# Block products of an MLP on one NeuronCore: another order of the products, operands split next to their use

## The chip, the cores and the metric

One core of a Trainium2 chip runs the kernel; the other cores are idle. The metric is the device time of one execution in microseconds (us). TensorE multiplies (moving operands stream through a stationary one, results in PSUM banks), VectorE and ScalarE work on tiles in SBUF and PSUM, SyncE (SP) issues the DMA transfers. Each engine works through its instructions in the order in which they stand in its queue, and waits where one needs something that isn't there.

## The reference, cut to what matters

```python
def reference(x, ..., w_out, norm_mlp_w, w_mlp_up, w_mlp_down, norm_final_w):
    ...
    h = h + mixed @ w_out
    hn = _rmsnorm(h, norm_mlp_w)
    h = h + jnp.square(jax.nn.relu(hn @ w_mlp_up)) @ w_mlp_down
    return _rmsnorm(h, norm_final_w)
```

h is 512 tokens by 2048, w_mlp_up is 2048 by 8192, w_mlp_down 8192 by 2048, all float32. Attention and the gated delta rule ahead of these lines are not touched by the change.

## The kernel before, in words

Up to about 1525 us the kernel computes the mixers and the output projection; then follow the MLP up (to about 2220 us), the MLP down (to about 2927 us) and the final norm.

Float32 products are made as three products of a reduced kind: an operand is split into a rounded half (hi, a cast on ScalarE, L94) and the rest (lo, a subtraction on VectorE, L95), and hi·lo, hi·hi and lo·hi are added up in PSUM (L902 to L904).

Both MLP projections are cut in blocks of two by two and multiplied by a scheme of seven products instead of eight. For a pair of output blocks the products are Q4, P1, P5, P6, P7, P3, P2. Each multiplies a weight block of 128x1024 (A11, A12, A22 as loaded, or one of the sums S1 to S4 that VectorE adds up at L909) with one of seven operands of eight tiles each: 11, 21, 22 as they are and T1 to T4, differences. In the trace weight halves are called wh_A, wl_A, wh_S, wl_S (and _u for up, _d for down), operands X_x and XT_x in up, X_h and XT_h in down. A weight block is split by `wsplit` into buffers of which there are three of each half. S2 is made from S1, and S4 from S2; S3 stands alone.

A product is 24 matmuls of 128x256: eight tiles by three. `BANK` says in which of three PSUM banks of a pair it is added up: P1, P6, P7 share one (b), P5 and P3 another (c), Q4 and P2 the third (a). P6, P7, P3 and P2 don't clear their bank but go on adding to what stands in it, so that what stood there must be copied out first where it is needed alone.

In up, `up_evac` does this: ScalarE copies the banks after Q4, P5, P1 and P6 into halves of two tiles tA and tB (L975 to L981), VectorE adds them to the banks after P7, P3 and P2, and relu with the norm's scale (L985, L994) and a square (L986, L995) give the hidden blocks r0 and r1. Then VectorE makes four differences of them (L999 to L1002), and all goes by DMA to a buffer hidD in HBM (L997 to L1005). There are 32 pairs in up: 0 and 1 together, 2 to 29 one by one, 30 and 31 together.

The down stage has four batches of hidden blocks; in each, four groups of two pairs of output blocks, with the products of the two pairs side by side. `operands(b)` loads 28 raw tiles of a batch (L1063, "hr", four buffers, shared with tA and tB) and splits them by `fill` into the operands, which have one buffer each. The h tiles of a group (four, of four buffers) are loaded from hTD in HBM (L1077), each product is added to them by VectorE, and they go back at P7 (h1) and P2 (h0) (L1115).

A scheduler puts the instructions of each engine in an order of its own, from dependences and from their order in the code; `pump` and `yield` feed tasks such as the statistic of the norm (`stat`, with its matmul L149 on the tile dg_h) between products.

## Time and profile before

| | |
|---|---|
| median of 3 runs | 2954.44 us (2952.85 to 2961.76) |
| the profiled execution | 2953.08 us, its span in the trace 2951.3 us |
| TensorE busy | 2831.7 us (96% of the span) |
| VectorE busy | 2070.7 us (70%) |
| ScalarE busy | 1167.5 us (40%) |
| DMA | 469.35 MB, 159 GB/s over the span |
| mean granted clock of TensorE | 0.988 of full speed |

The span is from the first to the last instruction of the trace. TensorE's matmuls overlap each other, so its busy time says little of how dense they stand; the distance from one start to the next does.

### The profile page before, as it was taken

To read this page: it belongs to the slowest core of one execution; us is meant where nothing else is said; L and a number is where in the kernel's file an instruction comes from. 1 tells how busy PE (TensorE), PEld (TensorE's weight loads), DVE (VectorE), ACT (ScalarE), POOL (GpSimd) and SP (SyncE) were. 2 spreads that over 40 slices of the span, in tenths; PEclk is the share of its full clock that TensorE was granted. 3 is DMA by queue.
4 is the path that set the end of the run, shared out by engine and by line. 5 is a ranking of instruction groups with operands and counts; after the bars stand their busy time and mean duration, and the time that the engine had idled before them with its cause. 6 is when DMAs were issued, how large, how long until landed. Compare 5 with 4: busy or idle time off the path is not lost.

```text
span 2951.3 us, 45595 instructions
## 1 busy us (share of the span) xinstructions
PE 2831.7 (96%) x17944; PEld 2547.0 (86%) x17944; DVE 2070.7 (70%) x3195; ACT 1167.5 (40%) x1869; POOL 24.8 (1%) x66
## 2 busy tenths in 40 slices
PE   8999999999999999999999999999997989989897
PEld 6778888888888888888879999999997989989897
DVE  6888779744554443444458878787788788888887
ACT  6443322233333333223344444444445353443543
POOL 0000000000000000000000000000000000000000
PEclk9999999999999999999999999999998999999998
DMA  7555653655632224443435444444447465555644
GB/s 231 190 186 186 220 174 116 223 157 172 184 109 91 94 85 145 155 148 121 147 113 171 144 145 132 153 129 147 140 142 235 155 213 172 188 185 175 207 139 143
DMA packets 217495, 469.35 MB, mean 159 GB/s; under 512 B 38976, under 2 KB 80000, under 8 KB 217280
## 3 DMA queue, kind: packets, MB, share of 16 engines
q1 hardware_dynamic: 216608, 464.33, 49.0%
q0 software_dynamic: 672, 2.10, 0.3%
q8 instruction: 141, 2.31, 0.3%
q14 instruction: 74, 0.61, 0.1%
HBM read 379.15 MB, written 87.20 MB: 158 GB/s over the span
## 4 chain that ended last, share of the span: by engine, by line
PE 76%; DVE 9%; DMA 8%; ACT 3%; issue 2%; SPq 0%; DVEq 0%; ACTq 0%
PE ps_b L902 12%; PE ps_b L904 11%; PE ps_b L903 11%; PE ps_mm L116 8%; PE ps_mm L115 8%; PE ps_mm L117 8%; PE ps_b L115 4%; PE ps_b L117 4%; PE ps_b L116 4%; DMA hr<-hidD 2%; ACT wh_S_u L94 1%; DMA bB<-rowD 1%; DMA Nd<-bB 1%; DVE wl_S_u L95 1%; DVE A_u L909 1%
## 5 line engine op out<-in xcount | busy, mean ns | idle before, releaser
L115 PE MATMUL ps_mm<-xh,wh_in 128*128 128x512 f32 x1416 | 566.6, 400 | 3.1 <-ACT wh_in L89 3.1
L117 PE MATMUL ps_mm<-xh,wl_in 128*128 128x512 f32 x1416 | 559.6, 395 | 0.4 <-DVE wl_in L90 0.4
L116 PE MATMUL ps_mm<-xl,wh_in 128*128 128x512 f32 x1416 | 559.2, 395 | 0.0
L89 ACT CAST wh_in<-raw_in 128x1024 fp32r<-128x1024 f32 x177 | 185.9, 1050 | 408.4 <-PE ps_mm L116 323.7
L117 PEld LDWEIGHTS ps_mm<-xh,wl_in 128*128 128x128 f32 x1416 | 267.0, 189 | 60.8 <-DVE wl_in L90 2.0
L115 PEld LDWEIGHTS ps_mm<-xh,wh_in 128*128 128x128 f32 x1416 | 267.3, 189 | 58.2 <-ACT wh_in L89 3.5
L116 PEld LDWEIGHTS ps_mm<-xl,wh_in 128*128 128x128 f32 x1416 | 267.4, 189 | 54.5 <-issue 0.2
L90 DVE TENSOR_TENSOR wl_in<-raw_in,wh_in 128x1024 fp32r<-128x1024 f32 x177 | 216.2, 1222 | 117.3 <-ACT wh_in L89 110.8
L902 PE MATMUL ps_b<-XT_x,wh_S_u 128*128 128x256 f32 x768 | 223.2, 291 | 13.7 <-ACT tA_u L979 13.5
L902 PE MATMUL ps_b<-XT_h,wh_S_d 128*128 128x256 f32 x768 | 221.1, 288 | 12.6 <-ACT wh_S_d L94 12.6
L904 PE MATMUL ps_b<-XT_h,wl_S_d 128*128 128x256 f32 x768 | 221.0, 288 | 0.8 <-DVE wl_S_d L95 0.8
L903 PE MATMUL ps_b<-XT_h,wh_S_d 128*128 128x256 f32 x768 | 220.9, 288 | 0.0
L904 PE MATMUL ps_b<-XT_x,wl_S_u 128*128 128x256 f32 x768 | 217.6, 283 | 0.0
L903 PE MATMUL ps_b<-XT_x,wh_S_u 128*128 128x256 f32 x768 | 217.6, 283 | 0.0
L94 ACT CAST wh_S_d<-A_d 128x1024 fp32r<-128x1024 f32 x124 | 129.9, 1048 | 190.3 <-PE ps_b L903 183.4
L95 DVE TENSOR_TENSOR wl_S_u<-A_u,wh_S_u 128x1024 fp32r<-128x1024 f32 x128 | 155.0, 1223 | 47.9 <-ACT wh_S_u L94 47.8
L94 ACT CAST wh_S_u<-A_u 128x1024 fp32r<-128x1024 f32 x128 | 132.9, 1050 | 137.8 <-DVE A_u L909 123.1
L95 DVE TENSOR_TENSOR wl_S_d<-A_d,wh_S_d 128x1024 fp32r<-128x1024 f32 x124 | 151.6, 1223 | 21.9 <-ACT wh_S_d L94 21.0
L902 PEld LDWEIGHTS ps_b<-XT_x,wh_S_u 128*128 128x128 f32 x768 | 147.1, 192 | 22.7 <-ACT tA_u L979 19.2
L902 PEld LDWEIGHTS ps_b<-XT_h,wh_S_d 128*128 128x128 f32 x768 | 151.1, 197 | 13.4 <-ACT wh_S_d L94 13.4
L902 PE MATMUL ps_b<-X_h,wh_A_d 128*128 128x256 f32 x512 | 146.6, 286 | 10.3 <-ACT wh_A_d L94 9.8
L904 PEld LDWEIGHTS ps_b<-XT_h,wl_S_d 128*128 128x128 f32 x768 | 151.2, 197 | 1.0 <-DVE wl_S_d L95 1.0
(393 smaller groups left out, 7063.8 us busy)
## 6 DMA issues: line engine op xcount, KB each, us to landing
raw_in<-in_win SPq DMA_DIRECT2D x177, 512.0 KB
raw_A_u<-in_wup SPq DMA_DIRECT2D x64, 512.0 KB
A_u<-in_wup SPq DMA_DIRECT2D x64, 512.0 KB
A_d<-in_wdn SPq DMA_DIRECT2D x64, 512.0 KB
raw_A_d<-in_wdn SPq DMA_DIRECT2D x64, 512.0 KB
raw_wo<-in_wout SPq DMA_DIRECT2D x32, 512.0 KB
h<-hTD SPq DMA_DIRECT2D x64, 256.0 KB
hTD<-h SPq DMA_DIRECT2D x60, 256.0 KB
```

The source lines that it names most:

```text
L89: S_.copy(out=hi, in_=raw)
L90: V.tensor_tensor(out=lo, in0=raw, in1=hi.bitcast(F32), op=ALU.subtract)
L94: S_.copy(out=hi, in_=src)
L95: V.tensor_tensor(out=lo, in0=src, in1=hi.bitcast(F32), op=ALU.subtract)
L115: PE.matmul(ps, hi[:, w], rh, start=first and kk == 0, stop=False)
L116: PE.matmul(ps, hi[:, w], rl, start=False, stop=False)
L117: PE.matmul(ps, lo[:, w], rh, start=False, stop=last and kk == 7)
L902: PE.matmul(ps, hi[:, c], t[:, lo_t], start=first and j == 0, stop=False, skip_group_check=True)
L903: PE.matmul(ps, hi[:, c], t[:, hi_t], start=False, stop=False, skip_group_check=True)
L904: PE.matmul(ps, lo[:, c], t[:, lo_t], start=False, stop=j == 7, skip_group_check=True)
L909: V.tensor_tensor(out=out, in0=x, in1=y, op=op)
```

## The change

The order of the seven products changes from Q4, P5, P1, P6, P7, P3, P2 to Q4, P1, P5, P6, P3, P7, P2, in up and down. The halves of tA and tB are dealt out anew, so that the two halves needed after P7 lie in one tile and one addition of 512 columns, with the bank broadcast, stands for two of 256. The four differences and the stores of a pair are put off (`late`) until the next pair has issued its third product. `operands(b)` no longer fills; `operand_fill` loads and splits one operand just ahead of the product of a batch's first group that reads it. The raw tiles have six buffers, not four. The statistic of the norm starts two steps and its matmul four steps later, and the tile of squares has one buffer.

```diff
-            sq = tp.tile([128, T], F32, tag="sq", name=f"sq{nm}", bufs=2)
+            sq = tp.tile([128, T], F32, tag="sq", name=f"sq{nm}", bufs=1)
...
-        def stat(nm, sq, cs=range(4)):
+        def stat(nm, sq, cs=range(4), wait=3, lead=0):
+            for _ in range(lead):
+                yield
...
-            yield from rstd_bcast(ps2, ps, nm, cs, 3)
+            yield from rstd_bcast(ps2, ps, nm, cs, wait)
...
-            ORDER = ("Q4", "P5", "P1", "P6", "P7", "P3", "P2")
+            ORDER = ("Q4", "P1", "P5", "P6", "P3", "P7", "P2")
...
                 elif q == "P5":
+                    S_.copy(out=tA[:, 1], in_=ps)
+                elif q == "P1":
                     S_.copy(out=tB[:, 0], in_=ps)
-                elif q == "P1":
-                    S_.copy(out=tA[:, 1], in_=ps)
...
                 elif q == "P7":
-                    add(r1[:, hi_t], ps, tB[:, 0])
-                    add(r1[:, lo_t], ps, tA[:, 0])
+                    add(r1.rearrange("p (o t) -> p o t", o=2), ps[:, None, :].to_broadcast([128, 2, 256]), tA)
...
+                late.append(lambda: differences(i, r0, r1, tA, tB))
+
+            late = []
+
+            def differences(i, r0, r1, tA, tB):
                 b, j = divmod(i, 8)
...
-            tasks.append(stat("h", sq))
+            tasks.append(stat("h", sq, wait=7, lead=2))
...
-                return sm.tile([128, 2, 256], F32, tag="et", name=name, bufs=4)
+                return sm.tile([128, 2, 256], F32, tag="et", name=name, bufs=6)
...
-                for q in order:
+                for n, q in enumerate(order):
                     for i, p in zip(idx, ps):
                         run_product(p, q, a_tile)
                         up_evac(i, p, q, et)
+                    if n == 2:
+                        while late:
+                            late.pop(0)()
...
             up_group((30, 31), ORDER)
+            while late:
+                late.pop(0)()
...
-                for o in ("T4", "T1", "11", "T2", "T3", "22", "21"):
-                    for j in range(0, 8, 2):
-                        raw = et(f"hr{b}{o}{j}")
-                        nc.sync.dma_start(out=raw, in_=hidD[b, OPS.index(o), :, j : j + 2, :])
-                        for e in range(2):
-                            fill(o, j + e, raw[:, e])
+
+            def operand_fill(b, o):
+                for j in range(0, 8, 2):
+                    raw = et(f"hr{b}{o}{j}")
+                    nc.sync.dma_start(out=raw, in_=hidD[b, OPS.index(o), :, j : j + 2, :])
+                    for e in range(2):
+                        fill(o, j + e, raw[:, e])
...
                 for q in order:
+                    if idx[0] == 0:
+                        operand_fill(b, ROLE[q])
                     for i, p in zip(idx, ps):
                         t = run_product(p, q, a_tile)
...
-                            add(h1[:, lo_t], h1[:, lo_t], t, ALU.subtract)
-                            add(h1[:, hi_t], h1[:, hi_t], t, ALU.subtract)
+                            hv = h1.rearrange("p (o t) -> p o t", o=2)
+                            add(hv, hv, t[:, None, :].to_broadcast([128, 2, 256]), ALU.subtract)
```

TensorE in an up pair (pair 3), at the joint of P3 (weights S4, operand 22) and P7 (weights S3, operand T3). Before, after 11 of the 24 matmuls of P3:

```order
L903 MATMUL ps_b_12930<-X22_x2_10857,wh_S4_u3_13050 128x256
L904 MATMUL ps_b_12930<-X22_x2_10857,wl_S4_u3_13051 128x256
L902 MATMUL ps_b_12930<-X22_x3_10858,wh_S4_u3_13050 128x256
L903 MATMUL ps_b_12930<-X22_x3_10858,wh_S4_u3_13050 128x256
L902 MATMUL ps_b_12960<-XT3_x0_12070,wh_S3_u3_13017 128x256
L903 MATMUL ps_b_12960<-XT3_x0_12070,wh_S3_u3_13017 128x256
```

and with the change, at the end of P3:

```order
L906 MATMUL ps_b_12948<-X22_x6_10861,wl_S4_u3_13015 128x256
L904 MATMUL ps_b_12948<-X22_x7_10862,wh_S4_u3_13014 128x256
L905 MATMUL ps_b_12948<-X22_x7_10862,wh_S4_u3_13014 128x256
L906 MATMUL ps_b_12948<-X22_x7_10862,wl_S4_u3_13015 128x256
L904 MATMUL ps_b_12917<-XT3_x0_12070,wh_S3_u3_13044 128x256
L905 MATMUL ps_b_12917<-XT3_x0_12070,wh_S3_u3_13044 128x256
```

Before, P7 stood whole inside P3, the other 13 matmuls of P3 behind it; now P3 is whole and P7 follows it.

VectorE in an up pair, between the differences of the pair before (tA, r0, tB) and the last weight half of the pair. Before (pair 27):

```order
L909 TENSOR_TENSOR tA_u26_18348<-r0_u26_18350 128x256
L909 TENSOR_TENSOR A22_u27_18551<-A22_u27_18551,raw_A11_u27_18547 128x1024
L1000 SCALAR_TENSOR_TENSOR tA_u26_18348<-tA_u26_18348,r1_u26_18351 128x256
L909 TENSOR_TENSOR r0_u26_18350<-r1_u26_18351,r0_u26_18350 128x256
L1001 SCALAR_TENSOR_TENSOR tB_u26_18349<-tA_u26_18348,r1_u26_18351 128x256
L95 TENSOR_TENSOR wl_S2_u27_18652<-A22_u27_18551,wh_S2_u27_18651 128x1024
L95 TENSOR_TENSOR wl_S3_u27_18682<-A21_u27_18552,wh_S3_u27_18681 128x1024
L909 TENSOR_TENSOR A22_u27_18551<-A22_u27_18551,raw_A12_u27_18549 128x1024
L95 TENSOR_TENSOR wl_S4_u27_18715<-A22_u27_18551,wh_S4_u27_18714 128x1024
```

and with the change (pair 28; line numbers move by two to six):

```order
L911 TENSOR_TENSOR A22_u28_18750<-A22_u28_18750,raw_A11_u28_18746 128x1024
L911 TENSOR_TENSOR tA_u27_18548<-r0_u27_18550 128x256
L1006 SCALAR_TENSOR_TENSOR tA_u27_18548<-tA_u27_18548,r1_u27_18551 128x256
L911 TENSOR_TENSOR r0_u27_18550<-r1_u27_18551,r0_u27_18550 128x256
L1007 SCALAR_TENSOR_TENSOR tB_u27_18549<-tA_u27_18548,r1_u27_18551 128x256
L95 TENSOR_TENSOR wl_S2_u28_18860<-A22_u28_18750,wh_S2_u28_18859 128x1024
L911 TENSOR_TENSOR A22_u28_18750<-A22_u28_18750,raw_A12_u28_18748 128x1024
L95 TENSOR_TENSOR wl_S4_u28_18890<-A22_u28_18750,wh_S4_u28_18889 128x1024
L95 TENSOR_TENSOR wl_S3_u28_18920<-A21_u28_18751,wh_S3_u28_18919 128x1024
```

S4 is added up (the second A22 line here) right behind the low half of S2 and ahead of the low half of S3; before it came behind both. The differences stand in about the same place.

The queue of SP at the end of up, around the last stores of pairs 30 and 31 (hidD written) and the first loads of the down stage's operands ("hr0T40" is batch 0, operand T4, tiles 0 and 1). Before:

```order
L1003 DMA hidD_94<-tA_u30_19300 128x2x256
L1004 DMA hidD_94<-tB_u30_19301 128x256
L1005 DMA hidD_94<-r0_u30_19302 128x256
L1077 DMA h0_1_19967<-hTD_93 128x512
L997 DMA hidD_94<-r0_u31_19336 128x256
L1063 DMA hr0T40_19783<-hidD_94 128x512
L1063 DMA hr0T42_19789<-hidD_94 128x512
L1003 DMA hidD_94<-tA_u31_19334 128x2x256
L1004 DMA hidD_94<-tB_u31_19335 128x256
L1005 DMA hidD_94<-r0_u31_19336 128x256
L1077 DMA h0_3_19969<-hTD_93 128x512
L1063 DMA hr0T44_19795<-hidD_94 128x512
```

and with the change:

```order
L1040 DMA A22_d0_3_20379<-in_wdn 128x1024
L1075 DMA hr0114_19871<-hidD_94 128x512
L82 DMA raw_A11_d0_1_19759<-in_wdn 128x1024
L1075 DMA hr0116_19877<-hidD_94 128x512
L1004 DMA hidD_94<-r1_u30_19264 128x2x256
L82 DMA raw_A12_d0_1_19761<-in_wdn 128x1024
L1075 DMA hr0T10_19943<-hidD_94 128x512
L1075 DMA hr0T12_19949<-hidD_94 128x512
L1004 DMA hidD_94<-r1_u31_19298 128x2x256
L1003 DMA hidD_94<-r0_u30_19263 128x256
L1009 DMA hidD_94<-tA_u30_19261 128x2x256
```

Before, the first of these loads came behind stores of pair 31; now the loads of T4, 11 and two of T1 stand ahead of pair 30's differences.

## Rows read from the trace of the kernel before

**Rows 1.** The head of the page: the span, and then for each engine the busy time, its share of the span and the instructions.

```profile
span 2951.3 us, 45595 instructions
...
PE 2831.7 (96%) x17944; PEld 2547.0 (86%) x17944; DVE 2070.7 (70%) x3195; ACT 1167.5 (40%) x1869; POOL 24.8 (1%) x66
```

**Rows 2.** The table by stretches, from 1525 us on: start and end, length, busy time and number of instructions of each engine, granted clock of TensorE, busy share of the DMA engines, GB/s. PEld is the load of the weights.

```profile
1560.00:1627.00 67.00, 65.15 (x537) 64.33 (x537) 55.70 (x71) 31.30 (x43) 0.00 (x0) 1.00 0.51 165
1627.00:2185.00 558.00, 537.35 (x4366) 526.36 (x4365) 440.13 (x546) 251.03 (x339) 0.00 (x0) 1.00 0.46 141
2185.00:2226.00 41.00, 34.97 (x292) 34.76 (x291) 34.39 (x44) 17.95 (x24) 0.00 (x0) 0.97 0.50 154
2226.00:2273.00 47.00, 35.73 (x242) 33.88 (x242) 39.42 (x84) 27.63 (x65) 0.00 (x0) 0.85 0.84 263
2273.00:2385.00 112.00, 111.58 (x919) 111.58 (x920) 91.79 (x111) 44.74 (x52) 0.00 (x0) 0.98 0.50 162
2385.00:2430.00 45.00, 36.29 (x273) 35.38 (x272) 39.99 (x81) 26.05 (x56) 0.00 (x0) 0.90 0.81 269
2430.00:2560.00 130.00, 130.00 (x1083) 130.00 (x1083) 106.77 (x131) 50.82 (x57) 0.00 (x0) 0.99 0.50 160
2560.00:2605.00 45.00, 36.12 (x268) 35.13 (x267) 39.49 (x79) 25.82 (x55) 0.00 (x0) 0.89 0.80 266
...
2728.00:2780.00 52.00, 42.41 (x324) 41.51 (x323) 45.88 (x88) 29.12 (x61) 0.00 (x0) 0.90 0.71 230
```

**Rows 3.** The waits of TensorE from 1500 to 2952 us: what stood, what it waited for, us in total, times, longest.

```profile
PE ps_b L902 <- ACT wh_S_d L94: 16.2, 6, 3.5
PE ps_b L902 <- ACT tA_u L979: 13.5, 28, 1.0
PE ps_b L902 <- ACT wh_A_d L94: 9.8, 3, 3.7
PE ps_b L902 <- ACT XT_h L94: 9.1, 2, 8.3
PE ps_b L904 <- DVE wl_S_u L95: 8.4, 13, 0.7
PE ps_b L904 <- DVE wl_A_d L95: 8.1, 4, 2.7
PE ps_b L149 <- DVE dg_h L145: 4.1, 1, 4.1
```

**Rows 4.** The chain of work in order of time, 1627 to 1720 us: start, length, what. One line of each period and one copy.

```profile
1627.21 1.06 ACT wh_S_u L94
...
1651.64 0.38 ACT tA_u L979
...
1670.18 1.06 ACT wh_S_u L94
...
1713.15 1.06 ACT wh_S_u L94
```

**Rows 5.** Two joints of products on TensorE in the up stage, from the trace in order of time: start, length of one (matmuls overlap), engine, line, operation, in brackets the idle time before and what ended it.

```profile
1633.32 0.28 PE L903 MATMUL ps_b<-X_x,wh_S_u 128*128 128x256 f32 x1
1634.25 0.39 PE L904 MATMUL ps_b<-X_x,wl_S_u 128*128 128x256 f32 x1 [0.65 <-DVE wl_S_u L95]
...
1651.33 0.28 PE L904 MATMUL ps_b<-X_x,wl_A_u 128*128 128x256 f32 x1
1652.07 0.39 PE L902 MATMUL ps_b<-XT_x,wh_S_u 128*128 128x256 f32 x1 [0.46 <-ACT tA_u L979]
```

**Rows 6.** Groups of instructions by line and shape, 1627 to 2185 us: out<-in, number | busy us, mean ns of one | idle before.

```profile
L95 DVE TENSOR_TENSOR wl_S_u<-A_u,wh_S_u 128x1024 fp32r<-128x1024 f32 x105 | 127.1, 1223 | 39.3 <-ACT wh_S_u L94 39.3
...
L94 ACT CAST wh_S_u<-A_u 128x1024 fp32r<-128x1024 f32 x105 | 108.9, 1050 | 108.0 <-DVE A_u L909 107.1 <-PE ps_b L903 0.9
L909 DVE TENSOR_TENSOR A_u<-A_u,raw_A_u 128x1024 f32<-128x1024 f32 x76 | 92.9, 1222 | 0.8
...
L985 DVE SCALAR_TENSOR_TENSOR r_u<-r_u,rB 128x512 f32<-128x512 f32 x26 | 18.0, 691 | 0.9
```

**Rows 7.** VectorE in order of time: two neighbouring wide operations in the down stage, then a row of 24 operand fills at the head of the up stage.

```profile
2381.00 1.22 DVE L909 TENSOR_TENSOR A_d<-A_d,raw_A_d 128x1024 f32<-128x1024 f32 x1
2382.14 0.41 DVE L909 TENSOR_TENSOR h<-ps_b,h 128x256 f32<-128x256 f32 x1
...
1537.33 8.13 DVE L95 TENSOR_TENSOR XT_x<-TRT,XT_x 128x256 fp32r<-128x256 f32 x24
```

**Rows 8.** Loads of operands and the casts that wait for them, in order of time: SP issues and ScalarE at batch 0, then the same at batch 1.

```profile
2230.33 1.74 SPq L1063 DMA_DIRECT2D hr0T<-hidD  x4
...
2233.90 1.34 ACT L94 CAST XT_h<-hr0T 128x256 fp32r<-128x256 f32 x4 [3.62 <-DMA hr0T<-hidD]
...
2388.32 0.32 SPq L1063 DMA_DIRECT2D hr<-hidD  x1
...
2392.67 0.71 ACT L94 CAST X_h<-hr 128x256 fp32r<-128x256 f32 x2 [0.18 <-DMA hr<-hidD]
```

**Rows 9.** The tail, in order of time: squares on ScalarE and their additions on VectorE.

```profile
2932.96 0.42 ACT L1165 ACTIVATE sqt<-h 128x256 f32<-128x256 f32 x1 [0.17 <-DVE sacc L909]
...
2932.51 1.47 DVE L909 TENSOR_TENSOR sacc<-sacc,sqt 128x256 f32<-128x256 f32 x3
```

**Rows 10.** The waits of the DMA queue of SP, 1500 to 2952 us, for reloads of h behind their stores.

```profile
SPq L1077 <- DMA hTD<-h: 101.6, 50, 4.2
```

More of the change, by code (lines that the diff above doesn't have):

```diff
@@ L989, in up_evac @@
                 else:
-                    add(r0[:, lo_t], ps, tA[:, 1])
+                    add(r0[:, lo_t], ps, tB[:, 0])
                 p.left -= 1
@@ L1163, in tail @@
                         m = 2 * (6 + k) + e
-                        sq = tp.tile([128, T], F32, tag="sq", name=f"sqt{m}{half}", bufs=2)
+                        sq = tp.tile([128, T], F32, tag="sq", name=f"sqt{m}{half}", bufs=1)
                         S_.activation(out=sq[:, ts], in_=h[:, ts], func=AF.Square)
```

## The prediction

> **What bounds the kernel now.** I read the page first: TensorE is busy for 2831.7 of 2951.3 us, VectorE for 70%, ScalarE for 40% [rows 1]. The change touches only what follows 1525 us, so the table by stretches came next [rows 2]. Its clean rows give the scale: from 2430 to 2560 us TensorE runs 1083 matmuls in 130.00 us, 0.12 us each. One product (24 matmuls) is 2.88 us, the seven of a pair 20.16 us, a down group of two pairs 40.32 us. Lost time of any stretch is then its length minus 0.12 us for each matmul; busy time hides part of it, because a late matmul is drawn longer.
>
> - Up, 1560 to 2185 us: 625 - 4903 x 0.12 = 36.6 us lost, at a granted clock of 1.00.
> - Start of the first down batch, 2185 to 2385 us: 200 - 1453 x 0.12 = 25.6 us.
> - Starts of the other batches: 45 - 273 x 0.12 = 12.2 us, 45 - 268 x 0.12 = 12.8 us, 52 - 324 x 0.12 = 13.1 us, with DMA at 0.71 to 0.81 and the clock at 0.90.
> - Inside a batch nothing: 2430 to 2560 us.
>
> The waits name the causes [rows 3]: bank copies (tA_u, 28 times, 13.5 us) and the low half of a sum (wl_S_u, 8.4 us) in up, operands and weight halves (XT_h, wh_S_d, wh_A_d, wl_A_d) at the batch starts. The chain shows the up loss as a period [rows 4]: the same cast starts at 1627.21, 1670.18 and 1713.15 us, so two pairs take 42.97 us and not 40.32: 2.65 us lost. Two kinds of stop make it. After P1 the next product P6 writes the same bank, and its first matmul comes 0.74 us after the one before it, waiting for L979; and every other pair P3's matmuls run ahead into a wait for wl_S_u (1633.32 to 1634.25 us) [rows 5].
>
> **The up pairs.** The new order puts another bank between any two products of one bank: b, c, b for P1, P5, P6, then c, b for P3, P7. The copy of P1 takes 0.38 us [rows 4] and starts behind the product's end and now has the 2.88 us of P5. The order of TensorE also no longer cuts P3 in two around P7. So both stops go, if the weights keep up. I walked one pair by hand, from the start T of Q4, along VectorE's new order with the durations of [rows 6] and the pitch of neighbouring operations in [rows 7] (a 1024-wide one every 1.13 us, a 256-wide one every 0.335 us, a cast 1.05 us). The sums are now a chain S1, S2, S4: P2 of the pair before ends at T; its last addition, the relu and the four differences stand between wl_S1 and wl_S2; S2's low half is ready at T + 7.0 us (P6 starts at T + 8.64), S4's at T + 10.5 (P3 starts at T + 11.52), S3's at T + 11.9 (P7 starts at T + 14.4). The thinnest slack is 1.0 us. VectorE is free twice after that, so no lateness builds up. I expect 20.2 us a pair and 35.5 of the 36.6 us back; the bounds are 30, if half of wl_S_u's 0.65 us waits survive, and 36.6. The single wide addition of P7 is priced between two 256-wide ones (0.67 us by pitch) and the 512-wide relu (0.69 us): nothing, since VectorE is not last there.
>
> The Trainium skill (TensorE: Matmul & The Clock Gate, the section on a second HAM failure mode) says that cycling through PSUM banks with short idle stretches can make the clock swing, so removing them would give back clock as well; by it the term would be larger. The granted clock of 1.00 through the up stage says that here nothing is to be had that way.
>
> **The batch starts.** Before, 28 raws of operands are filled through four buffers, all ahead of the weights of the first group. A fill is one cast and one subtraction of 256 columns; 56 of them cost VectorE 56 x 0.335 = 18.8 us. Now they stand next to their products, in the order of use, with six buffers. For batches 1 to 3 the queue of SP issues six raws during the batch before. The fills can start once the last group of a batch has used the first operand (after 5.76 us) and the last must be there before the first group's last product: 69 us of TensorE. VectorE works 82% of a group by busy time, 76% by pitch [rows 2, 7], so 52.5 + 18.8 = 71.3 us stand against 69 us, and weights split up to three ahead can hide the rest. Loss therefore 0.5 us with short landings. A load takes 3.6 us from its issue to the cast at batch 0 and 4.3 us at batch 1 [rows 8]; where a role's raws come one after another at 4 us, I get 5 us a batch. I take 3 us, since a DMA share of 0.8 will be spread but not gone: 38.1 - 9 = 29 us back (bounds 23 and 36.6).
>
> The Trainium skill (DMA: Bandwidth & Descriptors, Anatomy of one DMA) fits 2.0 us plus bytes over 436 GB/s to a transfer on another queue, an estimate of 2.6 us for 256 KB. By it the starts would lose 0.5 us each and the whole would come out at 2870 us; the rows with 3.6 and 4.3 us decide for the sum above.
>
> Batch 0 can't be prepared as far, since its last differences come from pairs 30 and 31. T4, 11 and half of T1 (ten raws) now land during the last up group, so the 8.3 us wait for the first XT_h [rows 3] goes. Left are 18 raws, 36 x 0.335 = 12.1 us of VectorE, with eight differences more (2.7 us) that now run after the group, and casts of later fills ahead of weight casts on ScalarE. My walk gives 9 us lost with landings of 2.7 us and 13.5 with 4 us. I take 12.5: 13 us back (bounds 5 and 18).
>
> **Small parts.** The later statistic of the norm: its matmul waited 4.1 us for dg_h [rows 3]. In the new order the small VectorE operations stand between fills, so dg_h comes some 4 us later, and products cover it: between 0 and 2 us back, I take 0. Late differences move VectorE work by three products, off the path; their stores move with them and are needed a batch later, so nothing, save for batch 0 above. One buffer for the squares: in the tail a square (0.42 us) must wait for the addition that reads the one before, twice or three times; from the rows [rows 9] I take 1 us slower (bounds 0 and 2).
>
> **Sum.** 35.5 + 29 + 13 - 1 = 76.5 us. The profiled execution takes 2953.08 us (span 2951.3), so 2876.6; the median of the runs is 1.36 us above it, so about 2878 us. The bounds of the terms together give 2859 to 2898.
>
> **Rivals.** (a) *Only the up stage gains.* VectorE is what the batch starts lack (71 against 69 us): if fills next to their use only move the stall from the start into the first group, 36 us come back and 2917 to 2919 us result. For it: casts of fills ahead of weight casts on ScalarE. Against: no more work is done there than before, and the loads begin a group earlier.
> (b) *Nearly every stall goes*: 1 us a batch, 5 at batch 0: 36 + 35 + 20 - 1 = 90, 2864 us or a little less. For it: DMA at 0.5 outside the starts. Against: the landings of [rows 8].
> (c) *The change doesn't do what it says in the up pairs.* S1, S2, S4 are adjacent; one more 1024-wide operation (1.13 us) ahead of wl_S4 uses up the slack of 1.0 us, and from 2.3 us late per pair nothing of the 1.32 us a pair is won. Then only 41 us of the down stage come back: about 2913 us. Against: the place of the four differences is already in the walk.
> (d) *Slower.* The h tiles of the down stage. h1 is stored after P7, now sixth and not fifth of the order, and Q4 of the next group adds into it first; h0's first addition, P1, is now second and not third. From the end of P7 (or P2) to the matching product of the next group there are 11.5 us for an addition (0.7), the wait of the reload behind the store (2.0 us on average, 4.2 at worst [rows 10]) and a load of 3.6 to 4.3: 2.3 to 5.2 us to spare. If SP's queue holds the reload back by more (weights and raws stand between), VectorE stops at the addition and the splits behind it wait, in 14 groups. It turns the whole slower when a group loses over 76/14 = 5.4 us, that is at reloads some 8 to 10 us later than now; 7 us a group would give 2975 us. Against: no loss at all inside batches today [rows 2].
>
> **How the numbers follow.** The sum above 0.55; (a) 0.16; (b) 0.15; (c) 0.08; (d) 0.06. A measurement of this kernel can tell about 0.3%, 9 us, from no change. (a), (b), (c) and the forecast are all faster by more; partial failures of several kinds leave 0.03 for no difference and (d) the rest. The likeliest case has its own range of 2859 to 2898; the one for 8 in 10 reaches up to (a) and (c), 2857 to 2918.
>
> **What would show it.** In the changed trace: no wait of P6's first matmul for a copy, and two pairs of up every 40.3 to 40.6 us, else the up term is wrong; the longest wait named then would be wl_S_u. 2 to 5 us lost in the 45 us around each batch start, with the clock near 1, and no 8 us stop at batch 0 but several of 1 to 3. Inside batches 0.12 us a matmul; a wait there for wh or wl behind an addition to h means (d). The forecast is wrong if the walk overlooked a queue, above all SP's, that starts a load later than its buffer allows.

## The result, and the profile after

The changed kernel takes 2883.99 us (median of 4 runs, 2876.94 to 2888.41), the kernel before on the same chip 2958.1 us (2952.85 to 2962.22): a ratio of 0.9748, with a 95% interval of 0.972 to 0.9776. That is 74 us less; 2878 us and a range of 2857 to 2918 us were forecast.

The profiled execution took 2884.02 us, its span 2881.9 us. The page's head, for [rows 1]:

```profile
span 2881.9 us, 45456 instructions
...
PE 2811.9 (98%) x17944; PEld 2538.3 (88%) x17944; DVE 2065.1 (72%) x3131; ACT 1167.0 (40%) x1869; POOL 24.8 (1%) x66
```

TensorE has the same 17944 matmuls and VectorE 64 operations less (one addition less after P7 in each of the 32 pairs of up and of down). The table by stretches answers to [rows 2]; the up stage starts 5 us later here, the down stage lies 40 to 70 us earlier. First 300 us of the up stage, then 46 us at the start of batch 0 and of batch 1, then the inside of a batch:

```profile
1800.00:2100.00 300.00, 300.00 (x2506) 300.00 (x2505) 254.01 (x299) 144.62 (x194) 0.00 (x0) 1.00 0.47 150
2188.00:2234.00 46.00, 37.14 (x266) 35.29 (x265) 40.99 (x77) 25.28 (x53) 0.00 (x0) 0.91 0.70 221
2365.00:2411.00 46.00, 43.73 (x354) 42.61 (x353) 43.06 (x68) 23.34 (x38) 0.00 (x0) 1.00 0.76 244
2420.00:2546.00 126.00, 126.00 (x1054) 126.00 (x1053) 107.72 (x149) 60.99 (x93) 0.00 (x0) 1.00 0.60 191
```

Up now runs without a gap: 2506 matmuls in 300.00 us are 0.12 us each. Batch 1 starts with 354 matmuls in 46 us (46 - 354 x 0.12 = 3.5 us lost) at a clock of 1.00; batch 0 with 266, 14 us lost, at 0.91 (more on this clock below, under the rest at batch 0). The waits of TensorE from 1500 us on answer to [rows 3]:

```profile
PE ps_b L904 <- ACT wh_S_d L94: 11.7, 11, 2.4
PE ps_b L904 <- ACT wh_A_u L94: 4.2, 1, 4.2
PE ps_b L906 <- DVE wl_S_d L95: 3.1, 6, 0.8
...
PE ps_s L1161 <- DVE sacc L911: 2.8, 1, 2.8
PE ps_b L149 <- DVE dg_h L145: 1.8, 1, 1.8
PE ps_b L906 <- DVE wl_S_u L95: 0.8, 1, 0.8
PE ps_b L904 <- ACT tB_u L983: 0.5, 1, 0.5
```

The 28 waits for a bank's copy are one, the 13 for wl_S_u [both rows 3] are one, the 8.3 us wait for XT_h is gone. What is left is mostly wh_S_d, the cast of a sum, at the batch starts (L902 to L904 are L904 to L906 now).

For all kernels below one ledger is used, taken from where the first matmul of each group starts in the trace (a down group has 336 matmuls, 40.32 us). "From up" is the time from the first matmul of up to the end of the span; what lies ahead is the same code in all of them and still differs (last section). "Up" is the time from there to the first down matmul beyond 32 x 20.16 = 645.1 us, in which the stage's head with the statistic and the first Q4 has some 12 us and, where there is one, the wait ahead of the first down matmul is counted too. The next four are the first group of each batch beyond 40.32 us; all other down groups lose under 0.5 us in every kernel, but for the very last, which runs into the tail.

| kernel | from up, us | up | batch 0 | 1 | 2 | 3 |
|---|---|---|---|---|---|---|
| before | 1425.9 | 57.7 | 17.8 | 13.1 | 13.3 | 13.5 |
| changed | 1351.3 | 12.7 | 15.3 | 3.8 | 2.9 | 4.9 |
| order alone | 1391.8 | 25.1 | 19.1 | 12.2 | 11.7 | 12.4 |
| old order in the changed kernel | 1396.0 | 49.1 | 16.3 | 6.5 | 5.7 | 7.3 |
| four raw buffers | 1367.5 | 26.8 | 10.3 | 7.7 | 5.5 | 5.8 |
| all fills ahead of the group | 1369.0 | 12.5 | 17.7 | 10.2 | 8.5 | 9.0 |
| P1 and P6 adjacent | 1382.5 | 43.6 | 15.8 | 3.7 | 3.6 | 4.7 |
| P6 and P7 adjacent | 1376.1 | 32.5 | 16.5 | 5.6 | 4.5 | 5.7 |
| sums ahead of fills | 1350.9 | 12.7 | 15.3 | 3.7 | 3.0 | 4.5 |
| pairs 30, 31 apart | 1355.7 | 13.6 | 19.0 | 4.0 | 3.2 | 4.2 |
| statistic as before | 1352.4 | 12.7 | 16.7 | 6.1 | 2.8 | 3.1 |
| eight raw buffers | 1345.9 | 13.4 | 13.7 | 2.4 | 2.5 | 2.8 |
| last differences later | 1352.0 | 12.6 | 17.2 | 2.9 | 4.6 | 3.6 |
| the same, eight buffers, tail | 1348.5 | 12.9 | 16.8 | 2.7 | 2.7 | 3.3 |

Before, 8.3 of the 57.7 us are the wait for the first XT_h [rows 3], so batch 0 cost 26.0 us there and up's pairs and head 49.4.

The ledger has one execution of each kernel. Four kernels have the same code in batches 1 to 3: changed, pairs 30, 31 apart, statistic as before, last differences later. Their single columns differ by up to 3.2 us, the sums over the three batches only from 11.1 to 12.0. So sums can be compared to about 1 us, single columns not.

### The profile page after: what moved, and what is told of

Read it like the earlier page. It is cut to its first block, busy times and chain, and to the rows that moved or that the text cites. A ratio compares the mean times of both kernels' runs of the same rounds, so it can differ in the third digit from the quotient of the medians.

```text
span 2881.9 us, 45456 instructions
## 1 busy us (share of the span) xinstructions
PE 2811.9 (98%) x17944; PEld 2538.3 (88%) x17944; DVE 2065.1 (72%) x3131; ACT 1167.0 (40%) x1869; POOL 24.8 (1%) x66
## 4 chain that ended last, share of the span: by engine, by line
PE 78%; DMA 9%; DVE 9%; ACT 2%; issue 1%; SPq 0%; DVEq 0%; ACTq 0%
PE ps_b L906 12%; PE ps_b L904 12%; PE ps_b L905 12%; PE ps_mm L115 8%; PE ps_mm L117 8%; PE ps_mm L116 8%; PE ps_b L115 4%; PE ps_b L116 4%; PE ps_b L117 4%; DMA hr<-hidD 1%; DVE wl_S_d L95 1%; DVE wl_in L90 1%; DMA bB<-rowD 1%; DMA hTD<-h 1%; DMA Nd<-bB 1%
## 5 line engine op out<-in xcount | busy, mean ns | idle before, releaser
L904 PE MATMUL ps_b<-XT_h,wh_S_d 128*128 128x256 f32 x768 | 220.8, 287 | 10.6 <-ACT wh_S_d L94 10.6
L906 PE MATMUL ps_b<-XT_h,wl_S_d 128*128 128x256 f32 x768 | 220.9, 288 | 3.2 <-DVE wl_S_d L95 3.1
L906 PE MATMUL ps_b<-XT_x,wl_S_u 128*128 128x256 f32 x768 | 217.4, 283 | 0.8 <-DVE wl_S_u L95 0.8
L904 PE MATMUL ps_b<-XT_x,wh_S_u 128*128 128x256 f32 x768 | 217.4, 283 | 0.5 <-ACT tB_u L983 0.5
L905 PE MATMUL ps_b<-XT_x,wh_S_u 128*128 128x256 f32 x768 | 217.3, 283 | 0.0
L904 PEld LDWEIGHTS ps_b<-XT_h,wh_S_d 128*128 128x128 f32 x768 | 149.8, 195 | 12.5 <-ACT wh_S_d L94 12.5
L906 PEld LDWEIGHTS ps_b<-XT_h,wl_S_d 128*128 128x128 f32 x768 | 149.9, 195 | 5.0 <-DVE wl_S_d L95 5.0
L905 PEld LDWEIGHTS ps_b<-XT_h,wh_S_d 128*128 128x128 f32 x768 | 149.9, 195 | 0.0
L906 PEld LDWEIGHTS ps_b<-XT_x,wl_S_u 128*128 128x128 f32 x768 | 147.2, 192 | 1.0 <-DVE wl_S_u L95 1.0
```

Source lines behind the costliest of these rows:

```text
L904: PE.matmul(ps, hi[:, c], t[:, lo_t], start=first and j == 0, stop=False, skip_group_check=True)
L905: PE.matmul(ps, hi[:, c], t[:, hi_t], start=False, stop=False, skip_group_check=True)
L906: PE.matmul(ps, lo[:, c], t[:, lo_t], start=False, stop=j == 7, skip_group_check=True)
```

## The experiments

### The order alone

```diff
 # on the kernel before
-            ORDER = ("Q4", "P5", "P1", "P6", "P7", "P3", "P2")
+            ORDER = ("Q4", "P1", "P5", "P6", "P3", "P7", "P2")
 # with the dealing of tA and tB and the wide addition of P7 in up, as in the change
```

> The kernel before with only the new order of the products, the dealing of tA and tB that goes with it and the single wide addition of P7; fills, four buffers, differences, statistic as before. If the parts add up, the up pairs run at 20.16 us each and every batch start loses its 25.6, 12.2, 12.8, 13.1 us as before: 35 to 36 us less than before, about 2921 us. Rival: without the late differences the chain S1, S2, S4 is late by 0.5 to 1 us a pair; then P3 waits for wl_S_u in most pairs and only 5 to 20 us come back, 2938 to 2953 us.

Measured: 2920.46 us (2918.49 to 2923.24), ratio 0.9866 (0.9851 to 0.9881). The stretch of up, as above:

```profile
1800.00:2100.00 300.00, 300.00 (x2507) 300.00 (x2506) 254.04 (x299) 145.01 (x195) 0.00 (x0) 1.00 0.47 150
```

2507 matmuls in 300.00 us: up is dense with the order alone. Neither late differences nor buffers are needed for that; the order of VectorE inside a steady pair is the same with and without `late`. The starts of batches 1 to 3 stay nearly as before (12.2, 11.7 and 12.4 us). Batch 0 gets worse: the wait ahead of the first down matmul is 11.7 us here and not 8.3, and the group behind it loses 19.1 us, 30.8 in all against 26.0. That the time meets the 2921 us forecast is partly luck: 5 us more at batch 0 stand against 3.6 us less at the three others.

### The fills and buffers alone

```diff
 # on the changed kernel
-            ORDER = ("Q4", "P1", "P5", "P6", "P3", "P7", "P2")
+            ORDER = ("Q4", "P5", "P1", "P6", "P7", "P3", "P2")
 # with the old dealing of tA and tB and two additions after P7 in up
```

> The changed kernel with the old order of the products (and its dealing of tA and tB and two additions after P7 in up); fills next to their use, six buffers, late differences stay. If the parts add up, up keeps its 2.65 us of loss for two pairs and the batch starts lose about 16, 3, 3 and 4 us as in the changed kernel: about 2920 us. Rival: the batch starts need the new order too; then they lose 8 us or more each, 2935 us or more.

Measured: 2923.27 us (2921.16 to 2930.61), ratio 0.9879 (0.9864 to 0.9894). Its longest entries in the waits of TensorE:

```profile
PE ps_b L904 <- ACT tA_u L981: 13.5, 28, 1.0
PE ps_b L904 <- ACT wh_S_d L94: 12.1, 13, 3.7
PE ps_b L906 <- DVE wl_S_u L95: 8.4, 13, 0.6
```

The two entries of up stand there again as in [rows 3], 13.5 us in 28 waits and 8.4 in 13. The batch starts lose 6.5, 5.7 and 7.3 us where the full change loses 3.8, 2.9 and 4.9. Neither half of the expectation held there: they lose more than the 3 to 4 us of the first and less than the 8 us of the rival. So the parts nearly add up: from the start of up, order alone saves 34.1 us, fills and buffers alone 29.9, both 74.6. The 10.6 us more are for the most part outside the steady pairs: 6.6 us in the ledger's four batch columns, since the batch starts gain more by the order once the fills are moved, and 3.4 us in the wait ahead of batch 0, which the order alone lengthens from 8.3 to 11.7 us and the fills take away. The late differences and the single buffer of squares were not run by themselves.

### Four raw buffers, and all fills ahead of the group

```diff
 # run 1, on the changed kernel
-                return sm.tile([128, 2, 256], F32, tag="et", name=name, bufs=6)
+                return sm.tile([128, 2, 256], F32, tag="et", name=name, bufs=4)
 # run 2, on the changed kernel
             def operands(b):
                 operand_tiles(OPS, f"h{b}_")
+                for q in ORDER:
+                    operand_fill(b, ROLE[q])
...
-                    if idx[0] == 0:
-                        operand_fill(b, ROLE[q])
```

> The changed kernel with four instead of six raw buffers. If the six are what lets the loads run ahead: the batch starts lose 8 to 12 us each and the time goes to 2900 to 2915 us. Rival: the place of the fills next to their products is enough: within 4 us of the changed kernel's 2884 us.

> The changed kernel, six buffers, but all 28 raws of a batch are loaded and split ahead of its first group, as before (in the new order of operands). If the place of the fills is what counts, fills stand ahead of weight splits in the queues again and the starts of batches 1 to 3 lose about 12 us each, 2910 to 2920 us. Rival: the two more buffers are what counts: 2884 to 2892 us.

Measured: 2899.59 us with four buffers (2898.17 to 2900.63, ratio 0.9794), 2903.72 us with the fills ahead (2902.05 to 2906.46, ratio 0.981). Both parts count, each for 16 to 18 us from the start of up, at different places. With four buffers there is one stop ahead of batch 0:

```profile
PE ps_b L904 <- ACT XT_h L94: 14.3, 1, 14.3
```

tA and tB of pairs 30 and 31 hold all four: the last store of the two is issued at 2195.68 us, the first raw's load at 2197.74. Behind the stop the first group loses 5.0 us less than in the changed kernel, so that 9 of the 16 us are batch 0's and 7 the other starts', which lose 5.5 to 7.7 us and not the 8 to 12 expected. With the fills ahead, batches 1 to 3 lose 8.5 to 10.2 us, less than the 12 expected and more than the rival has; 2903.72 us lies between the two ranges. The two more buffers may be what makes 8.5 to 10.2 out of 12; that isn't shown by itself.

### One adjacency of a bank at a time

```diff
 # run 1, on the changed kernel: P6 behind P1 again
-            ORDER = ("Q4", "P1", "P5", "P6", "P3", "P7", "P2")
+            ORDER = ("Q4", "P5", "P1", "P6", "P3", "P7", "P2")
 # run 2, on the changed kernel: P7 behind P6 again
-            ORDER = ("Q4", "P1", "P5", "P6", "P3", "P7", "P2")
+            ORDER = ("Q4", "P1", "P5", "P6", "P7", "P3", "P2")
```

> The changed kernel with P1 and P5 swapped in the order (Q4, P5, P1, P6, P3, P7, P2), so that P6 follows P1 on the same bank again, while P3 stays whole ahead of P7. If the shared bank is what cost, each single pair loses 0.7 us at the joint of P1 and P6 (a wait for a copy of 0.4 to 0.5 us) and nothing else, 20 us in all: about 2904 us. Rival: what cost was P7 cutting P3 in two; then nothing comes back, 2882 to 2887 us.

> The changed kernel with P3 and P7 exchanged (Q4, P1, P5, P6, P7, P3, P2): P7 follows P6 on its bank again, P6 no longer P1. On TensorE 7 or 8 matmuls of P3 now run ahead of P7 and the rest behind it, as before the change. If that cut costs by itself (a wait for a low half of a sum of 0.65 us), 15 to 25 us come back: about 2904 us. If only lateness of the sums cost, and S4 and S3 are ready at 10.5 and 11.9 us after Q4's start as in the changed kernel, nothing comes back: 2881 to 2887 us.

Measured: 2916.32 us (2911.04 to 2924.72, ratio 0.9867) for P1 and P6, 2912.04 us (2908.65 to 2914.06, ratio 0.9843) for P6 and P7. Up loses 30.9 and 19.8 us more than in the changed kernel; in the steady pairs Q4 follows Q4 every 21.25 and 20.87 us there, 20.13 in the changed kernel. Neither stop looks as expected. The entry of each in the waits of TensorE, run 1 and then run 2:

```profile
PE ps_b L904 <- ACT wh_S_u L94: 22.8, 27, 1.1
```

```profile
PE ps_b L906 <- DVE wl_S_u L95: 12.8, 26, 0.8
```

That is one such stop in nearly every one of the 28 single pairs, and it waits for a weight half and not for a copy. (The idle time before the matmul is less than what a pair loses: the next matmuls come late too.) The joint behind P1 in run 1, TensorE in order of time:

```profile
1652.31 0.28 PE L906 MATMUL ps_b<-X_x,wl_A_u 128*128 128x256 f32 x1
1653.42 0.39 PE L904 MATMUL ps_b<-X_x,wh_S_u 128*128 128x256 f32 x1 [0.83 <-ACT wh_S_u L94]
1653.65 0.28 PE L905 MATMUL ps_b<-X_x,wh_S_u 128*128 128x256 f32 x1
1653.77 0.31 PE L904 MATMUL ps_b<-XT_x,wh_S_u 128*128 128x256 f32 x1
```

Behind P1 come two matmuls of P3 (X_x with a sum: operand 22), and only then P6 (XT_x): the scheduler has put P3's first matmuls into the joint where P6 would have to wait for the bank, and they wait 0.83 us for the cast of S4. That cast ends 9.6 us after Q4's start, here as in the changed kernel; there P3 starts at 11.5 us, here its first matmuls are wanted at 8.6. In run 2, VectorE and TensorE around the joint behind P6:

```profile
1656.21 2.44 DVE L95 TENSOR_TENSOR wl_S_u<-A_u,wh_S_u 128x1024 fp32r<-128x1024 f32 x2 [0.16 <-ACT wh_S_u L94]
1658.57 1.22 DVE L911 TENSOR_TENSOR A_u<-A_u,raw_A_u 128x1024 f32<-128x1024 f32 x1
1660.96 1.23 DVE L95 TENSOR_TENSOR wl_S_u<-A_u,wh_S_u 128x1024 fp32r<-128x1024 f32 x1 [1.17 <-ACT wh_S_u L94]
```

```profile
1661.56 0.28 PE L904 MATMUL ps_b<-X_x,wh_S_u 128*128 128x256 f32 x1
1661.68 0.28 PE L905 MATMUL ps_b<-X_x,wh_S_u 128*128 128x256 f32 x1
1662.24 0.39 PE L906 MATMUL ps_b<-X_x,wl_S_u 128*128 128x256 f32 x1 [0.28 <-DVE wl_S_u L95]
```

P3's first matmuls again stand in the joint, but now S4 is made behind S3: two low halves in a row (S2 and S3), then the sum S4 at 1658.57 and its low half at 1660.96, ready at 1662.19, while P3 began at 1661.56. So in both runs the stop hangs on a weight, not on the copy itself: with two products of a bank in a row the scheduler fills the joint with matmuls of P3, whose weights, S4, aren't ready: in run 1 they are wanted a product earlier, in run 2 they are made later, behind S3. The order of the sums follows the order of the products; that S4 and S3 would stay ready at 10.5 and 11.9 us, as the second half of the expectation has it, was wrong. How much the bare wait for a copy would cost without such filling isn't shown by these two; in the kernel before, where P6 did wait for it, it was 13.5 us in 28 waits [rows 3], 0.48 us each. (Of the products that "The kernel before, in words" lists as adding to their bank, P2 does clear it: it stands in the code's `FIRST`. The joints tested here are of P6 and P7, which don't.)

### The rest at the start of batch 0

Four edits were aimed at the 15 us that batch 0 still loses.

```diff
 # run 1: in a batch's first group, sums and splits of a product's weights ahead of the fills
+                        ws = [weights(p, q, a_tile) for p in ps]
+                        operand_fill(b, ROLE[q])
 # run 2: pairs 30 and 31 one after the other
-            for i in range(2, 30):
+            for i in range(2, 32):
                 up_group((i,), ORDER)
-            up_group((30, 31), ORDER)
 # run 3: eight raw buffers ("et"), six tiles of sums ("a") instead of seven
 # run 4: late.pop(0)() of pairs 30 and 31 behind P3 of the first down group
```

> The changed kernel, but in the first group of a batch the sums and splits of a product's two weight blocks stand ahead of the fills of its operand in the code. If fills ahead of sums on VectorE and ahead of weight casts on ScalarE make the rest of the batch starts (16 us at batch 0, about 3 at the others), batch 0 loses 8 to 10 and the others 1 to 2: 2872 to 2878 us. Rival: the late loads make it; then it stays within 3 us of 2884 us, or a little above, since operands come later.

> The changed kernel with pairs 30 and 31 of up one after the other and not together. Together their tA and tB hold four of the six raw buffers until their differences are made, so that batch 0's loads go through two. If that makes batch 0's 16 us, it falls to 8 to 11 us: 2877 to 2880 us. Rival: fills ahead of weights in the queues make it: no change, 2882 to 2886 us.

> The changed kernel with eight raw buffers instead of six, paid for with one tile of weight sums less (six, not seven). If batch 0's 15 us come from raws that wait for a buffer while tA and tB of pairs 30 and 31 hold four, they fall to 8 to 10 us and the other starts from 3 to 5 to about 2: 2872 to 2878 us. Rival: it is VectorE that lacks time there; then the starts stay within 1 us of before and the time at 2882 to 2886 us. If six tiles are too few for the weights, every group loses and the time is above 2890 us.

> The changed kernel, but the differences of pairs 30 and 31, which only batch 3 reads, are made and stored behind the product P3 of the first down group and not ahead of the group. If VectorE's queue at the start of batch 0 is what lacks (eight differences there, 2.7 us, and stores of theirs ahead of raws in SP's queue), the 15 us of batch 0 fall to 9 to 11 us, the rest stays: 2877 to 2880 us. Rival: the work is only moved within the first group, where VectorE lacks time up to its end: 14 to 16 us, 2883 to 2886 us.

Measured: 2886.21 us (2882.93 to 2889.06), 2890.29 us (2884.54 to 2896.05), 2875.21 us (2874.38 to 2876.07, ratio 0.972 with 0.9706 to 0.9735) and 2885.38 us (2882.27 to 2887.6). Batch 0 loses 15.3, 19.0, 13.7 and 17.2 us; none comes down to the 8 to 11 us that the four expectations start with. By the whole time runs 1, 2 and 4 can't be told from the changed kernel (ratios 0.9763, 0.9775 and 0.9752 against 0.9748, and the intervals overlap). Run 1 came out as its rival. Run 2 lies above both of its ranges: there the first raw of batch 0 is asked for 13 us ahead of the first down matmul, in the changed kernel 29 us; that this makes the 19.0 isn't shown. Run 3 lies in its range of time but not for its reason: the ledger gives it 5.4 us and not 6 to 12, the rest of the 8.8 us between the medians lies ahead of up (1526.7 and 1530.6 us in the profiled executions) or between the runs.

In runs 1 and 3 TensorE's waits at batch 0 change their name and not their sum, 8.8 and 8.7 us, 8.8 in the changed kernel. TensorE from 2180 to 2235 or 2240 us, first the changed kernel, then sums ahead of fills:

```profile
PE ps_b L904 <- ACT wh_S_d L94: 8.6, 8, 2.4
```

```profile
PE ps_b L905 <- DVE XT_h L95: 4.0, 5, 1.2
PE ps_b L905 <- DVE X_h L95: 1.7, 1, 1.7
PE ps_b L904 <- ACT wh_S_d L94: 1.6, 2, 1.3
PE ps_b L904 <- ACT X_h L94: 1.5, 1, 1.5
```

With the sums first, TensorE waits for operands instead of weights. Two raw buffers more bring 1.6 us at batch 0, not 5 to 7, which one execution can't tell from nothing (changed and statistic as before, the same code there, have 15.3 and 16.7), and 4 us at the three other starts together. So neither the place of the fills against the sums nor the number of buffers is the bound there. Nor is it VectorE's work alone: in these 46 us it is busy for 40.99 us, and at batch 1, with a fourth of the loss, for 43.06 us.

Run 4 is another case. Nearly all its waits at batch 0 are one stop that the changed kernel hasn't:

```profile
PE ps_b L904 <- DVE h L911: 14.4, 2, 13.9
```

TensorE waits for additions to h; how the late differences bring that about is shown with the last run below. So run 4 doesn't tell whether VectorE's queue is what lacked.

A part of the 15.3 us is the clock, for which my sum had no term. In the changed kernel's batch 0 (a stretch of 16 us, then TensorE in order of time):

```profile
2204.00:2220.00 16.00, 12.52 (x81) 12.11 (x80) 13.38 (x26) 9.19 (x25) 0.00 (x0) 0.79 0.56 180
```

```profile
2211.12 0.39 PE L904 MATMUL ps_b<-XT_h,wh_S_d 128*128 128x256 f32 x1 [2.40 <-ACT wh_S_d L94]
2211.35 0.28 PE L905 MATMUL ps_b<-XT_h,wh_S_d 128*128 128x256 f32 x1
2212.71 0.58 PE L904 MATMUL ps_b<-XT_h,wh_S_d 128*128 128x256 f32 x1 [1.08 <-ACT wh_S_d L94]
2213.08 0.42 PE L906 MATMUL ps_b<-XT_h,wl_S_d 128*128 128x256 f32 x1
2213.30 0.42 PE L904 MATMUL ps_b<-XT_h,wh_S_d 128*128 128x256 f32 x1
2213.52 0.41 PE L905 MATMUL ps_b<-XT_h,wh_S_d 128*128 128x256 f32 x1
```

Behind stops of 2.40 and 1.08 us the matmuls come 0.21 us apart and not 0.12: the lower of the clock's two levels, 1.2 and not 2.4 GHz. Some 40 matmuls of batch 0's first group run so and cost 3.8 us (counted are matmuls that start more than 0.2 us after the one before and not right behind a wait); 8.8 us are waits, the other 2.7 the matmuls right behind a wait. In batch 1's first group hardly one runs so. In the first groups of the four batches it is some 145 matmuls before the change and 60 with it, 13.5 and 5.5 us: of the 39 us that the change brings at the batch starts, 8 are clock.

What else batch 0 has and batch 1 hasn't is the end of two up pairs in the same queues; which link of the chain from raw, fill and sum to cast sets its waits stays open.

The last run put differences, buffers and the tail together (eight raw buffers, the squares of the tail in raw buffers):

> The same with eight raw buffers and six tiles of sums, and the squares of the tail in raw buffers, which stand empty there. By the run with eight buffers alone the starts of batches 1 to 3 lose 2.4 to 2.8 us. If the late differences and the buffers add up at batch 0, it loses 6 to 9 us and not 13.7; the tail wins 0.7 us: 2867 to 2871 us. Rival: tA and tB are held longer, so that batch 0 stays at 12 to 14 us: 2873 to 2876 us.

Measured: 2882.7 us (2879.03 to 2884.4), ratio 0.9739 (0.9724 to 0.9753); batch 0 loses 16.8 us, more than either half of the expectation has, and the time is above both ranges. TensorE, VectorE and SP in order of time:

```profile
2207.46 0.28 PE L906 MATMUL ps_b<-XT_h,wl_S_d 128*128 128x256 f32 x1
2220.06 0.55 PE L904 MATMUL ps_b<-X_h,wh_S_d 128*128 128x256 f32 x1 [12.32 <-DVE h L911]
```

```profile
2215.22 0.42 DVE L1007 SCALAR_TENSOR_TENSOR tB_u<-tA_u,r_u 128x256 f32<-128x256 f32 x1
```

```profile
2215.66 0.32 SPq L1087 DMA_DIRECT2D h<-hTD  x1
```

and SP's first load of an h tile in the changed kernel:

```profile
2193.46 0.42 SPq L1089 DMA_DIRECT2D h<-hTD  x1
```

The first h tile is asked for 22 us later. The h tiles use the same four buffers as r0 and r1 of the last pairs, which the late differences still read: the last difference that reads r1 of one of these pairs ends at 2215.64 us, and the load follows at 2215.66. The additions to h wait, the banks stay full, and TensorE stops for 12.32 us. In run 4 above it is the same: the first h tile is asked for at 2210.66 us, and the stop is 13.9 us. The tail did win: the last group and what follows it take 60.9 us, 62.6 in the changed kernel and 61.9 in most others with the changed tail.

Of all versions the one with eight raw buffers is the fastest, by 5.4 us from the start of up in the ledger; the intervals of its ratio and of the changed kernel's still overlap.

### The statistic as before

```diff
-            tasks.append(stat("h", sq, wait=7, lead=2))
+            tasks.append(stat("h", sq, wait=3, lead=0))
```

> The changed kernel with the statistic of the norm as before (no lead, three steps). In the changed kernel TensorE stands 1.8 us for dg_h and 4.2 us for the first wh_A_u of up, before 4.1 and 1.4 us. Expected: 4 us for dg_h and 1.4 us for wh_A_u again, the first matmul of Q4 21 to 22 us after the first of up as before and not 20.5; at most 1.5 us in the whole.

Measured: 2882.4 us in one run. The waits are 4.1 us for dg_h and 1.0 us for wh_A_u, and Q4 of up starts 21.51 us after the first matmul, 20.55 in the changed kernel and 21.73 before: 1 us, as expected. But it doesn't last: where Q4 of both first pairs has ended, 144 matmuls after the start, TensorE is behind 0.12 us a matmul by 11.9 us here, 12.0 in the changed kernel and 12.1 before, and "up" in the ledger is 12.7 us with both. In the changed kernel Q4 begins, behind its wait of 4.2 us, at the lower level of the clock:

```profile
1551.00:1556.50 5.50, 4.89 (x21) 4.60 (x22) 5.31 (x5) 2.18 (x3) 0.00 (x0) 0.50 0.98 398
```

## Why the prediction was right

- **Up pairs: 35.5 us forecast, 36.5 measured** (49.4 to 12.7 is 36.7, with 0.2 of it at the head). Both stops went, and two pairs take 40.26 us (40.3 to 40.6 forecast). The walk of one pair held nearly to the tenth: in a pair whose Q4 starts at 1806.04 us, TensorE has P6 at 1814.6 and P3 at 1817.52, and VectorE's lines are

```profile
1811.98 1.22 DVE L95 TENSOR_TENSOR wl_S_u<-A_u,wh_S_u 128x1024 fp32r<-128x1024 f32 x1
1813.23 1.23 DVE L911 TENSOR_TENSOR A_u<-A_u,raw_A_u 128x1024 f32<-128x1024 f32 x1
1815.62 2.45 DVE L95 TENSOR_TENSOR wl_S_u<-A_u,wh_S_u 128x1024 fp32r<-128x1024 f32 x2 [1.17 <-ACT wh_S_u L94]
```

  S2's low half ends 7.2 us after Q4's start (7.0 forecast), S4's, the first of the two in the last line, at about 10.8 (10.5): 0.7 us ahead of P3 instead of 1.0. Rival (c) didn't come, but its slack is thin; the run with P6 and P7 adjacent shows what one 1024-wide operation ahead of S4 does (0.74 us a pair).
- **Batches 1 to 3: 3 us each forecast, 3.8, 2.9 and 4.9 measured**; 28.3 us back where 29 were forecast. The 3 us were a choice between 0.5 and 5 and not a working, so that it is so near is partly luck. The estimate of 2.6 us a load by the Trainium skill's fit for another queue (DMA: Bandwidth & Descriptors, Anatomy of one DMA) gave 0.5 us each; the 3.6 and 4.3 us of the rows were nearer.
- **Batch 0: 13 us forecast, 10.7 back** (26.0 to 15.3). The size was right within its bounds, the reason partly wrong. I wrote that batch 0 can't be prepared as far because its last differences come from pairs 30 and 31. Pairs 0 to 7 make batch 0's hidden blocks; 30 and 31 make some of batch 3's. What they hold is the raw buffers (four of the six), the buffers of h and VectorE's queue. The picture was the one forecast: no 8 us stop, several smaller ones, the longest 2.4 us. 3.8 of the 15.3 us still lost are matmuls at the clock's lower level, which the sum didn't count.
- **Head: 0 forecast, 0.2 back.** Q4 starts 1.2 us earlier, and the run above puts 1.0 of it down to the statistic; by the end of Q4 all but 0.2 us is lost again.
- **Tail: 1 us slower forecast, 1.2 measured** (61.4 to 62.6 us from the start of the last group to the end). The wait for sacc went from 2.0 to 2.8 us; the other kernels with the same tail need 61.9 to 62.6 us, so between 0.5 and 1.2 us is the tail's.
- **Sum: 76.5 us forecast, 74.6 from the start of up, 74 by the medians.** Up pairs 1 us better and batch 0 2.3 us worse than forecast nearly cancel. The spans differ by 69.4 only, since the profiled execution reached up at 1530.6 us and the one before at 1525.4, in stages which the change doesn't touch but for a buffer.
- **Rivals (a) and (b)** lie on both sides of what came: 39 us came back at the batch starts where (a) had none, and 26.9 us are still lost there where (b) had 8.
- **Rival (d)** didn't come: inside batches every matmul takes 0.12 us, and SP's waits for a reload behind its store fell from 101.6 [rows 10] to 66.5 us:

```profile
SPq L1089 <- DMA hTD<-h: 66.5, 48, 4.5
```

- **The clock.** Up's granted clock was 1.00 before, with stops of 0.46 and 0.65 us in it [rows 5], and is 1.00 now; nothing came back there, as forecast. The Trainium skill (TensorE: Matmul & The Clock Gate, the section on a second HAM failure mode) tells of a kernel whose short idle stretches between groups of matmuls make the clock swing; this trace shows no swing with those of up. At batch 1 the granted clock was 0.90 with three stops of 2.7 to 3.1 us, and is 1.00 with three of 0.4 to 1.1 us.

## What to carry to other kernels

Where two products in a row add to one accumulator that has to be copied out between them, put a product of another bank there, and look at what a scheduler puts into the joint if you don't: here it was matmuls whose weights weren't ready yet. Move the sums with the products, for the order in which weights are made decides whether the new joint is covered, and walk one period by hand with durations from the trace. At a change of stage, ask which buffers the old stage still holds (here raws, h tiles) before moving its last work later. And price a stop by more than its wait: behind some of those at the batch starts the matmuls came 0.21 us apart for a while, and not 0.12.

## What was not expected

The stages ahead of up, the same instructions but for one buffer of squares, took between 1525.4 and 1535.7 us in the fourteen profiled executions, with no order by kernel (before 1525.4, changed 1530.6, eight buffers 1526.7, fills ahead 1535.7; the two with two buffers of squares, before and order alone, 1525.4 and 1529.7). That is more than several of the effects measured here; the sums above are therefore taken from the start of up. It arises ahead of 1000 us: by then TensorE has run 4820 matmuls in the kernel before, 4800 in the changed one and 4774 with the fills ahead, while from 1000 to 1500 us the three run 2224 or 2225 each. The granted clock is 0.99 to 1.00 in all of these stretches; what makes the difference stays open.
